# Attention's second stage: shares one step sooner, residual loads spread, last transposes and values one step sooner

## Chip, cores and metric

The kernel runs on one core of one Trainium2 chip, as one launch. The metric is the device time of a whole execution in microseconds, the median of several runs. Before the change it was 2018.47 us (three runs, 2016.84 to 2018.92).

## What is computed

Two layers of a decoder trunk over 1024 tokens of 1024 channels, all in float32: a gated short convolution, then a dilated sliding-window attention with 16 heads of 64 channels and three dilation groups. The change touches the attention layer only. There every head has three groups of queries, keys and values; each group gives an output and the logarithm of its softmax denominator, and the three outputs are added with weights (the shares) made from these denominators:

```python
def dilated_attention_mixer(h, w_in, q_gain, k_gain, w_out, rel_bias):
    proj = h @ w_in
    ...
    for g, (window, dilation) in enumerate(DILATED_GROUPS):   # (128, 1), (512, 4), (2048, 16)
        ...
        o, l = dilated_group_attention(q, k, qkv[:, :, g, 2], bias_g, window, dilation)
        outs.append(o)
        lses.append(l)
    alpha = jax.nn.softmax(jnp.stack(lses, axis=0), axis=0)
    o = jnp.sum(alpha[..., None] * jnp.stack(outs, axis=0).astype(jnp.float32), axis=0)
    y = o.reshape(B, S, ATTN_WIDTH).astype(h.dtype) * jax.nn.silu(z)
    return y @ w_out                                          # and x + y @ w_out is the result
```

## The kernel before

The first 1640 us compute the convolution layer and attention's projections. They leave queries and keys (`qkd`), values (`vd`), the SiLU gate (`zd`), the residual stream (`x1d`) and the skewed position biases (`sk0` to `sk2`) in device memory. From about 1640 us on runs the second stage, which alone is changed.

It treats the 16 heads as 8 pairs (`hp` 0 to 7), each pair as three units (`g` 0 to 2), and each unit as steps: 4, 4 and 2. So a pair has 10 steps and the stage 80, numbered 0 to 79; the last steps of the pairs are 9, 19, ... 79. A step has three parts, made by `make`:

- A: scores. TensorE multiplies queries and keys (L888, tile `ps`), VectorE adds the bias and takes the maximum (L896, tiles `xs` and `nl`), ScalarE takes the exponential and its sum (L899).
- B: TensorE transposes the probabilities (L906, tile `pt`); ScalarE or VectorE copies them to SBUF (L846, L844, tile `pts`).
- C: TensorE multiplies them with the values (L925, L919 for `g` 2, tile `po`); after a unit's last step VectorE copies the output out (`finish`, L936).

Engines run their instructions in the order in which the program was written. That order is fixed by hand: a loop counts k from 0, and at each k it issues every piece whose step plus lag is k. A has lag 0, B has lag `LB` = 2, C lag `LC` = 4. Within one k the lags come in the order 0, 1, 4, 3, 5 to 14, 2. After these come `extra` (the output projection, below) and `begins` (loads). Before all of them `add_sums` adds finished projections to the residual.

After a pair's last step (`end`) hangs a chain that joins its three groups; its pieces are functions inside `attention`, and their lags are counted from that last step:

- `store` (L942, L944, L947): `nl` of groups 0 and 1 goes to `nld` in device memory, in another order; at group 2 all of it is loaded back as `ml`. The DMAs are issued by GpSimd.
- `weights` (L956 to L960): maxima and exponentials on VectorE and ScalarE. `shares` (L969 to L974): the quotients, tile `fo`.
- `store_shares` (L977) sends them to `fd`, and `spread(w)` (L982, two DMAs) loads them back, repeated over 64 partitions, as `fb`. There are two `fb` buffers, so `spread(0)` waits for `scale(2)`.
- `scale(w)` (L985, VectorE, 1024 columns), `add(w)` (L988, GpSimd), `gate` (L991), `high` and `low` (L995, L998).

Before the change the lags of a pair that isn't the last are: `store` 1, `weights` 3, `shares`, `store_shares`, `spread(2)`, `spread(1)` 4, `scale(2)` and `spread(0)` 8, `scale(1)` and `add(2)` 9, `scale(0)` and `add(0)` 11, `gate` 12, `high` 13, `low` 14. GpSimd's queue holds these DMAs and the adds in that order, and an instruction that waits there holds up all behind it. So do the other engines' queues.

The last pair goes without device memory: `wide` (L1007, L1009) widens the shares on chip, `spread_last` (L1017) transposes them with TensorE into `ps` banks, and `last` multiplies, adds and gates half a row at a time.

The output projection lies between the steps: `some` multiplies two pairs' outputs with the output weights for one tile of 128 channels by 512 tokens, six matmuls (L1066 to L1068), in a PSUM bank (`pd`, of which there is one; `ps` has three, `pt` two, `po` two). There are three rounds of 16 such tiles: at k 34 to 49, at 54 to 69, and from 74 on, where six tiles are done by 79 and the rest at the stage's end, two to a k. `add_sums` (L1102) adds each to `acc`, which was loaded with the residual by `residual` (L1083, SyncE's queue) at k 4 to 19. `fetch`, `split` and `split_low` (L1077, L1080) prepare output weights. After the loop five tiles get pair 6's and 7's part in two goes (`first`), and eleven the whole.

The two lines that place the stores and the joining, and the one that places the loads:

```python
            end.setdefault(1, []).append(store)
...
                    todo = [(3, weights), (LC, shares), (LC, store_shares), (LC, lambda: spread(2)),
...
            when(4 + i, residual, dt, hf)
```

Of the kernel before, what the change touches and what calls it, by code (L numbers as in the profile page):

```python
# [35 lines left out]
def trunk(ctx: ExitStack, tc: tile.TileContext, a, out):  # L36
# [98 lines left out]
    with tc.tile_pool(name="wq", bufs=1) as wq, tc.tile_pool(name="sle", bufs=1) as sle, \  # L135
# [197 lines left out]
        with tc.tile_pool(name="rp", bufs=1, side="right") as rp, tc.tile_pool(name="cp", bufs=2, side="right") as cp, \  # L333
# [62 lines left out]
            with tc.manual_schedule(engines={mybir.EngineType.Activation}):  # L396
                ps, T = {}, {}
# [107 lines left out]
        with tc.tile_pool(name="ev", bufs=1, side="right", reuse_waits="tile") as ev, tc.tile_pool(name="xb", bufs=1, side="right", reuse_waits="tile") as xb, \  # L505
# [35 lines left out]
            WO, ps = {}, {}  # L541
# [268 lines left out]
    with tc.tile_pool(name="sp", bufs=3, space=PSUM) as sp, tc.tile_pool(name="ptp", bufs=2, space=PSUM) as ptp, \  # L810
# [37 lines left out]
        def attention(hp, g):  # L848
# [130 lines left out]
            def spread(w):  # L979
                fb = u["fb", w] = fbp.tile([P, S], F32, name="fb", tag="fb")  # L980
                for s, hs in enumerate((lo, up)):
                    nc.gpsimd.dma_start(fb[hs], fd[hp, w, s][None, :].to_broadcast([64, S]))  # L982

            def scale(w):
                nc.vector.tensor_tensor(O[hp, w], O[hp, w], u["fb", w], op=OP.mult)  # L985
# [25 lines left out]
            def spread_last(hf):  # L1011

                hs = slice(64 * hf, 64 * hf + 64)
                for w in (2, 1, 0):
                    fb = u["fb", w] = sp.tile([P, 4, P], F32, name="ps", tag="ps").rearrange("p a b -> p (a b)")
                    for r in range(8):
                        nc.tensor.transpose(fb.rearrange("p (i r) -> p r i", r=8)[:, r],  # L1017
                                            u["wide", w][hs, r * P:r * P + P], ident[hs, hs])

            def last(hf, i):  # L1020
                h, z = half(hf), SZ[hp][:, half(hf)]
                if i == 0:
                    for w in (2, 1, 0):
                        nc.vector.tensor_tensor(O[hp, w][:, h], O[hp, w][:, h], u["fb", w], op=OP.mult)
                elif i == 1:
                    for w in (2, 0):
                        nc.vector.tensor_tensor(O[hp, 1][:, h], O[hp, 1][:, h], O[hp, w][:, h], op=OP.add)
                    nc.vector.tensor_tensor(z, O[hp, 1][:, h], z, op=OP.mult)
                    if hf == 0:
                        y2[hp] = [ap.tile([P, S], F32R, name="qk", tag="qk", bufs=6) for _ in range(2)]  # L1030
                    nc.scalar.activation(y2[hp][0][:, h], z, AF.Copy)
                else:
                    nc.vector.tensor_tensor(y2[hp][1][:, h], z, y2[hp][0][:, h].bitcast(F32), op=OP.subtract)

            steps = []
# [3 lines left out]
                    st = make(js, not steps)  # L1039
                    steps.append({lag: [f] for lag, f in zip((0, LB, LC), st)})  # L1040
            end = steps[-1]
            end.setdefault(1, []).append(store)
            if g == 2:
                if hp == HP - 1:
                    todo = [(LB, weights), (3, shares), (3, wide), (LC, lambda: spread_last(0)),
                            (LC, lambda: last(0, 0)), (LC, lambda: last(0, 1))]
                    ending.update(spread=spread_last, last=last)
                else:
                    todo = [(3, weights), (LC, shares), (LC, store_shares), (LC, lambda: spread(2)),
                            (LC, lambda: spread(1)), (8, lambda: scale(2)), (8, lambda: spread(0)),  # L1050
                            (9, lambda: scale(1)), (9, lambda: add(2)), (11, lambda: scale(0)),
                            (11, lambda: add(0)), (12, gate), (13, high), (14, low)]
                for lag, f in todo:
                    end.setdefault(lag, []).append(f)
# [59 lines left out]
        def when(k, f, *x):  # L1114
            begins.setdefault(k, []).append(lambda: f(*x))
# [1 line left out]
        for un, (k, prefetch) in at.items():  # L1117
            when(max(0, k - 2), load_v, *un)
        for i, (dt, hf) in enumerate(tiles):
            when(4 + i, residual, dt, hf)  # L1120
        for r in range(3):
            k0 = at[2 * r + 2, 0][0] + LD
            k = k0
            for i, (dt, hf) in enumerate(tiles):
                late = k >= len(steps)
                name = "pd" if not late else ("pd", ("ps", "ps", "pt", "pt")[min(k - len(steps), 3)])[i % 2]
                extra.setdefault(k, []).append(lambda r=r, dt=dt, hf=hf, name=name:
                                               some((2 * r, 2 * r + 1), dt, hf, name))
                k += i % 2 if late else 1
        for kt in range(KT):  # L1130
            k = at[kt // 2 * 2 + 2, 0][0] + LD - 4 + kt % 2 if kt < 6 else len(steps) - 5 + kt % 2
            when(k - 4 - kt % 2, fetch, kt)
            when(k, split, kt)
            when(k + 1, split_low, kt)
        for f in begins.pop(-1):
            f()
        k = 0
        while k < len(steps) + LC or any(x >= k for x in extra):
            add_sums()
            for lag in (0, 1, LC, 3, *range(LC + 1, 15), LB):  # L1140
                for f in steps[k - lag].get(lag, ()) if 0 <= k - lag < len(steps) else ():
                    f()
            for f in extra.get(k, ()):
                f()
            for f in begins.get(k, ()):
                f()
            k += 1
# [94 lines left out]
```

## Time and profile before

| | us |
|---|---|
| median of three runs | 2018.47 |
| lowest, highest | 2016.84, 2018.92 |
| the profiled execution | 2009.19 |
| its span, first to last instruction | 2007.3 |
| TensorE busy in the span | 1948.4 (97%) |
| VectorE, ScalarE, GpSimd busy | 1482.8, 903.7, 881.5 |

The profile is one execution, about 9 us shorter than the median; differences are worked out on it and laid on the median. TensorE is busy 97% of the span; the rest are idle stretches, and within the busy time some stretches run at a lower granted clock. In the page's strip of 40 slices, TensorE shows 9 (90% or more) nearly everywhere; 8 stands in slices 35 to 38 and in the last one, that is in the stage that is changed and at the very end. A timeline row ends in square brackets when its engine sat idle before it: for how long, and which instruction ended the wait.

### The profile page before, as it was taken

What the parts mean: (1) busy time and instruction counts of PE and PEld (TensorE: products, weight loads), DVE (VectorE), ACT (ScalarE), POOL (GpSimd) and SP (SyncE); (2) the same over time, 40 slices, a digit from 0 to 9 for tenths busy, and PEclk for the clock granted to TensorE, in tenths of its full rate; (3) what the DMA queues carried; (4) which work ended last, traced back from release to release, by engine and by line L of the source; (5) the groups of instructions that cost most, each with busy time, mean ns of one, the idle gap of its engine ahead of it and who ended that gap; (6) DMA issues with size and microseconds to landing.
All of it is one profiled execution on the core that took longest, in us unless ns stands there. A gap on an engine that the chain in (4) does not pass through costs nothing.

```text
span 2007.3 us, 29480 instructions
## 1 busy us (share of the span) xinstructions
PE 1948.4 (97%) x10302; PEld 1583.3 (79%) x10302; DVE 1482.8 (74%) x2751; ACT 903.7 (45%) x2042; POOL 881.5 (44%) x800
## 2 busy tenths in 40 slices
PE   8999999999999999999999999999999998899998
PEld 6888778888888888788888888888888876677776
DVE  6866576566666655788889788968898856687886
ACT  5433233333334444444434443344333348777670
POOL 0356566666664211344445444544444441322230
PEclk9999999999999999999999999999999999999999
DMA  5326512122113564323333233323323368757752
GB/s 192 116 67 143 145 60 74 69 69 74 69 69 127 193 227 161 127 89 106 105 116 116 84 106 116 116 80 109 116 95 102 109 216 268 215 153 216 215 153 85
DMA packets 116805, 254.25 MB, mean 127 GB/s; under 512 B 15822, under 2 KB 22718, under 8 KB 116656
## 3 DMA queue, kind: packets, MB, share of 16 engines
q1 hardware_dynamic: 93024, 177.42, 26.9%
q0 software_dynamic: 23632, 74.95, 13.1%
q8 instruction: 81, 1.33, 0.3%
q14 instruction: 68, 0.56, 0.1%
HBM read 193.05 MB, written 67.64 MB: 130 GB/s over the span
## 4 chain that ended last, share of the span: by engine, by line
PE 66%; DVE 10%; issue 5%; DMA 2%; ACT 2%; POOL 1%; DVEq 0%; POOLq 0%; ACTq 0%; SPq 0%
PE pp L299 16%; PE pp L301 15%; PE pp L302 15%; PE pp L550 3%; PE pp L551 3%; PE pp L549 3%; PE ps L888 2%; DVE ws L165 2%; PE pt L906 2%; PE po L925 2%; DVE blkc L706 1%; DVE ri L67 1%; DMA nld<-nl 1%; ACT xs L899 1%; DVE st L670 1%
## 5 line engine op out<-in xcount | busy, mean ns | idle before, releaser
L165 DVE TENSOR_TENSOR ws<-wr,ws 128x512 fp32r<-128x512 f32 x284 | 268.4, 947 | 126.8 <-ACT ws L164 125.4
L164 ACT ACTIVATE ws<-wr 128x512 fp32r<-128x512 f32 x284 | 178.4, 630 | 389.5 <-PE pp L302 235.7
L164 ACT ACTIVATE ws<-sr 128x512 fp32r<-128x512 f32 x272 | 169.7, 629 | 293.8 <-PE pp L302 238.5
L274 POOL TENSOR_TENSOR sr<-wr 128x512 f32<-128x512 f32 x136 | 185.1, 1361 | 258.2 <-DVE rit L66 76.3
L165 DVE TENSOR_TENSOR ws<-sr,ws 128x512 fp32r<-128x512 f32 x272 | 235.7, 873 | 81.3 <-ACT ws L164 79.6
L311 DVE TENSOR_TENSOR f<-pp,f 128x512 f32<-128x512 f32 x204 | 139.5, 684 | 84.6 <-PE pp L302 80.0
L899 ACT ACTIVATE xs<-xs,nl 128x128 f32<-128x128 f32 (+1 forms) x384 | 167.9, 439 | 68.4 <-DVE nl L896 57.3
L307 ACT ACTIVATE f<-pp 128x512 f32<-128x512 f32 x228 | 132.5, 581 | 26.8 <-POOL blkc L678 12.9
L896 DVE CUSTOM_DVE_ANT_0 xs<-ps,bt 128x128 f32<-128x128 f32 (+1 forms) x384 | 110.8, 347 | 26.1 <-PE ps L888 16.4
L711 POOL DMA_DIRECT2D qkd<-blkc x96 | 68.1, 716 | 134.1 <-DVE blkc L706 126.7
L274 POOL TENSOR_TENSOR sr<-wr,sr 128x512 f32<-128x512 f32 x68 | 89.1, 1310 | 81.4 <-issue 57.7
L669 ACT ACTIVATE f<-f 128x512 f32<-128x512 f32 x96 | 60.7, 633 | 139.0 <-DVE f L311 101.8
L299 PE MATMUL pp<-blke,ws 128*128 128x512 f32 x272 | 108.2, 398 | 6.8 <-ACT f L307 6.8
L299 PE MATMUL pp<-blkg,ws 128*128 128x512 f32 x272 | 107.6, 396 | 4.6 <-ACT f L307 3.7
L301 PE MATMUL pp<-blkg,ws 128*128 128x512 f32 x272 | 106.8, 393 | 3.3 <-DVE blkg L519 3.3
L299 PE MATMUL pp<-blkf,ws 128*128 128x512 f32 x272 | 108.6, 399 | 0.7 <-ACT f L307 0.7
L299 PE MATMUL pp<-blka,ws 128*128 128x512 f32 x272 | 107.2, 394 | 0.7 <-ACT f L307 0.7
L299 PE MATMUL pp<-blkb,ws 128*128 128x512 f32 x272 | 107.5, 395 | 0.0
L301 PE MATMUL pp<-blke,ws 128*128 128x512 f32 x272 | 107.4, 395 | 0.0
L302 PE MATMUL pp<-blke,ws 128*128 128x512 f32 x272 | 107.1, 394 | 0.0
L299 PE MATMUL pp<-blkd,ws 128*128 128x512 f32 x272 | 107.0, 394 | 0.0
L302 PE MATMUL pp<-blkg,ws 128*128 128x512 f32 x272 | 106.5, 391 | 0.0
(329 smaller groups left out, 5387.6 us busy)
## 6 DMA issues: line engine op xcount, KB each, us to landing
wr<-in_conv_w_in SPq DMA_DIRECT2D x128, 256.0 KB, 2.8
wr<-in_wqk SPq DMA_DIRECT2D x96, 256.0 KB, 3.0
qkd<-blkc POOLq DMA_DIRECT2D x96, 256.0 KB, 3.1
qk<-qkd SPq DMA_DIRECT2D x48, 512.0 KB, 8.5
wr<-in_conv_w_out SPq DMA_DIRECT2D x64, 256.0 KB, 3.1
f<-in_x SPq DMA_DIRECT2D x48, 256.0 KB, 4.6
wr<-in_wv SPq DMA_DIRECT2D x48, 256.0 KB, 2.9
vd<-f POOLq DMA_DIRECT2D x48, 256.0 KB, 2.5
```

The costliest lines, as they stand in the source:

```text
L164: nc.scalar.activation(t[:, 0], src, AF.Copy)
L165: nc.vector.tensor_tensor(t[:, 1], src, t[:, 0].bitcast(F32), op=OP.subtract)
L274: nc.gpsimd.tensor_tensor(t, x, y, op=op)
L299: nc.tensor.matmul(ps, w[:, 0, ws], b[:, k, 0], start=new and k == 0, stop=False, skip_group_check=not new)
L301: nc.tensor.matmul(ps, w[:, 0, ws], b[:, k, 1], start=False, stop=False, skip_group_check=not new)
L302: nc.tensor.matmul(ps, w[:, 1, ws], b[:, k, 0], start=False, stop=end and k == 3, skip_group_check=not new)
L307: nc.scalar.activation(t, ps, AF.Copy)
L311: nc.vector.tensor_tensor(m, ps, m, op=OP.add)
L669: nc.scalar.activation(sq, t, AF.Square)
L711: nc.gpsimd.dma_start(qkd[hp, g, which].rearrange("p (c s) -> p c s", c=c) [:, :, hf * m:(hf + 1) * m], o.rearrange("p (c s) -> p c s", c=c))
L896: nc.vector.tensor_tensor_reduce(out=x, in0=ps[s][:, x0:x0 + nk].rearrange("p a b -> p (a b)"), in1=u["bt"][s][:, bs], op0=OP.add, op1=OP. ...
L899: nc.scalar.activation(x, x, AF.Exp, bias=nm, scale=-1.0, accum_out=L)
```

## The change

It moves pieces to other places and renames banks; it adds and removes no arithmetic.

- `store` of group 2 (the load of `ml`) from lag 1 to 0.
- For pairs 0 to 6: `weights` from lag 3 to 2 (at the end of that k, after B), `shares`, `store_shares`, `spread(2)` and `spread(1)` from 4 to 3.
- For pair 7: B of step 79 and `weights` go to the end of k = 80 (by `begins`), C of steps 78 and 79 from lag 4 to 3, `shares` and `wide` from 3 to 2, `spread_last(0)` and the first two parts of `last` from 4 to 3. The loop ends one k sooner.
- `residual` at k 6, 8, ... 36 in place of 4 to 19.
- In every round the tiles 14 and 15 use a `po` bank in place of `pd`; in the third round the last four tiles stand together at k = 83, with the banks in another order.

```diff
-            end.setdefault(1, []).append(store)
+            end.setdefault(0 if g == 2 else 1, []).append(store)
             if g == 2:
                 if hp == HP - 1:
-                    todo = [(LB, weights), (3, shares), (3, wide), (LC, lambda: spread_last(0)),
-                            (LC, lambda: last(0, 0)), (LC, lambda: last(0, 1))]
-                    ending.update(spread=spread_last, last=last)
+                    steps[-2][3] = steps[-2].pop(LC)
+                    end[3] = end.pop(LC)
+                    todo = [(2, shares), (2, wide), (3, lambda: spread_last(0)), (3, lambda: last(0, 0)),
+                            (3, lambda: last(0, 1))]
+                    ending.update(turn=end.pop(LB)[0], weights=weights, spread=spread_last, last=last)
                 else:
-                    todo = [(3, weights), (LC, shares), (LC, store_shares), (LC, lambda: spread(2)),
-                            (LC, lambda: spread(1)), (8, lambda: scale(2)), (8, lambda: spread(0)),
+                    todo = [(LB, weights), (3, shares), (3, store_shares), (3, lambda: spread(2)),
+                            (3, lambda: spread(1)), (8, lambda: scale(2)), (8, lambda: spread(0)),
...
-            when(4 + i, residual, dt, hf)
+            when(6 + 2 * i, residual, dt, hf)
...
-                name = "pd" if not late else ("pd", ("ps", "ps", "pt", "pt")[min(k - len(steps), 3)])[i % 2]
+                name = "pd" if not late else (("pd", "ps"), ("pd", "ps"), ("pd", "pt"), ("pt", "pd"))[
+                    min(k - len(steps), 3)][i % 2]
+                if i >= 14:
+                    name = "po"
...
-                k += i % 2 if late else 1
+                k += (i % 2 if i < 13 else 0) if late else 1
...
+        when(len(steps), ending["turn"])
+        when(len(steps), ending["weights"])
...
-        while k < len(steps) + LC or any(x >= k for x in extra):
+        while k < len(steps) + LC - 1 or any(x >= k for x in extra):
```

VectorE's queue at pair 2, from the gate of pair 1 (k = 31) to the scores of step 32. (`sz` is the gate's tile, `wraw` a raw output weight whose low part L1080 makes.) Before:

```order
L936 COPY o<-po 128x512
L991 TENSOR_TENSOR sz<-o,sz 128x1024
L1080 TENSOR_TENSOR y_14810<-wraw,y_14810 128x1024
L896 ISA xs,nl<-ps,bt 128x256
L896 ISA nl 128x1
```

The same place after the change:

```order
L991 TENSOR_TENSOR sz<-o,sz 128x1024
L956 TENSOR_TENSOR mx<-ml 128x16
L957 TENSOR_TENSOR mx<-mx,nl 128x16
L958 TENSOR_TENSOR f<-mx,ml 128x8x4
L959 TENSOR_TENSOR f<-mx,nl 128x8x2
L1082 TENSOR_TENSOR y_14807<-wraw,y_14807 128x1024
L896 ISA xs,nl<-ps,bt 128x256
L896 ISA nl 128x1
```

The four instructions of `weights`, the first of which needs `ml`, now stand ahead of the scores of step 32.

The same queue behind the scores of step 32. Before, the copies out of `po` at k = 33 (two L936) come next but four scores, and `shares` only behind them:

```order
L956 TENSOR_TENSOR mx<-ml 128x16
L957 TENSOR_TENSOR mx<-mx,nl 128x16
L958 TENSOR_TENSOR f<-mx,ml 128x8x4
L959 TENSOR_TENSOR f<-mx,nl 128x8x2
L844 COPY pts<-pt 128x384
L1080 TENSOR_TENSOR y_14853<-wraw,y_14853 128x1024
L896 ISA xs,nl<-ps,bt 128x256
```

After the change, VectorE behind the scores of step 32:

```order
L969 TENSOR_TENSOR den<-f,ml 128x8x4
L970 TENSOR_TENSOR den<-f,nl 128x8x2
L971 TENSOR_TENSOR den<-den 128x8x2
L972 TENSOR_TENSOR mx<-den 128x16
L973 RECIPROCAL mx<-mx 128x16
L974 TENSOR_TENSOR fo<-f,mx 128x8x6
L844 COPY pts<-pt 128x384
L1082 TENSOR_TENSOR y_14857<-wraw,y_14857 128x1024
L896 ISA xs,nl<-ps,bt 128x256
```

`shares` has moved from behind the scores and copies of k = 33 to ahead of the copy L844 of k = 32.

TensorE's queue at the end of k = 80 and the start of k = 81 (the first row is the end of a projection tile). Before:

```order
L1068 MATMUL ps<-y_17144,y_17097 128x512
L925 MATMUL po<-pts,V 64x128 x8
L906 MATMUL pt<-ident,xs 128x128 x8
L1066 MATMUL pd<-y_16575,y_17054 128x512
L1067 MATMUL pd<-y_16575,y_17054 128x512
```

After the change, TensorE from the end of the same projection tile on:

```order
L1070 MATMUL ps<-y_17159,y_17104 128x512
L906 MATMUL pt<-ident,xs 128x128 x8
L925 MATMUL po<-pts,V 64x128 x8
L919 MATMUL po<-pts,V 64x64 x16
L1068 MATMUL pd<-y_16590,y_17054 128x512
```

B of step 79 has moved ahead of C of step 77, and C of step 78 (L919) stands right behind that, with no projection between them. GpSimd's queue holds the same instructions in the same order before and after; only the loop's k differ.

## Rows read from the trace of the kernel before

**Rows 1.** Stretches: us, busy us (and instructions) of each engine, clock, DMA share, GB/s.

```profile
1685.00:1765.00 80.00, 67.14 (x702) 52.11 (x699) 57.15 (x253) 61.34 (x232) 23.51 (x26) 0.89 0.74 209
1765.00:1830.00 65.00, 65.00 (x599) 50.03 (x597) 52.23 (x211) 45.82 (x185) 20.56 (x24) 1.00 0.78 222
...
1950.00:1978.00 28.00, 24.86 (x201) 19.66 (x200) 20.13 (x40) 7.62 (x21) 2.77 (x2) 0.94 0.01 3
```

**Rows 2.** Timeline of TensorE: start, us, operation, [idle before, what ended it].

```profile
1702.59 2.07 PE L888 MATMUL ps<-qk 64*128 64x128 f32 x14 [4.21 <-DVE nl L896]
...
1740.11 2.07 PE L888 MATMUL ps<-qk 64*128 64x128 f32 x14 [3.88 <-DVE nl L896]
...
1758.22 1.61 PE L888 MATMUL ps<-qk 64*128 64x256 f32 x6 [2.99 <-DVE nl L896]
...
1845.50 0.88 PE L925 MATMUL po<-pts,V 128*64 128x128 f32 x12 [0.30 <-DVE o L936]
...
1952.62 1.14 PE L906 MATMUL pt<-ident,xs 128*128 128x128 f32 x8 [0.80 <-ACT pts L846]
...
1973.46 0.56 PE L1066 MATMUL pd<-y,y 128*128 128x512 f32 x1 [2.34 <-DVE acc L1102]
1973.82 0.63 PE L1067 MATMUL pd<-y,y 128*128 128x512 f32 x1
```

**Rows 3.** Timeline of VectorE, k = 12 to 23.

```profile
1681.12 0.17 DVE L956 TENSOR_TENSOR mx<-ml 128x16 f32<-128x16 f32 x1
...
1685.32 0.18 DVE L969 TENSOR_TENSOR den<-f,ml 128x32 f32<-128x32 f32 x1
...
1700.47 1.23 DVE L985 TENSOR_TENSOR o<-o,fb 128x1024 f32<-128x1024 f32 x1 [4.60 <-DMA fb<-fd]
...
1717.22 0.42 DVE L896 CUSTOM_DVE_ANT_0 xs<-ps,bt 128x256 f32<-128x256 f32 x1
...
1722.25 0.18 DVE L969 TENSOR_TENSOR den<-f,ml 128x32 f32<-128x32 f32 x1
```

**Rows 4.** Timeline of VectorE, k = 27 to 33.

```profile
1737.98 1.23 DVE L985 TENSOR_TENSOR o<-o,fb 128x1024 f32<-128x1024 f32 x1 [4.29 <-DMA fb<-fd]
...
1755.12 1.22 DVE L991 TENSOR_TENSOR sz<-o,sz 128x1024 f32<-128x1024 f32 x1 [2.59 <-POOL o L988]
...
1757.39 0.42 DVE L896 CUSTOM_DVE_ANT_0 xs<-ps,bt 128x256 f32<-128x256 f32 x1
...
1762.36 1.28 DVE L936 COPY o<-po 128x512 f32<-128x512 f32 x2
```

**Rows 5.** Timeline of GpSimd: issues of `nld` and `ml` for pairs 0, 2 and 4.

```profile
1674.37 0.56 POOL L942 DMA_DIRECT2D ml<-nld  x1 [6.86 <-issue]
...
1740.55 1.55 POOL L947 DMA_DIRECT2D nld<-nl  x2
...
1752.13 0.57 POOL L942 DMA_DIRECT2D ml<-nld  x1 [6.89 <-DVE nl L896]
...
1834.54 0.57 POOL L942 DMA_DIRECT2D ml<-nld  x1 [6.77 <-DVE o L985]
```

**Rows 6.** Tile `ml`, all pairs: its load, from issue to landing.

```profile
DMA to landing us min/median/max: 1.9/4.1/6.1
```

**Rows 7.** Tile `ml`, 1751 to 1753 us (pair 2).

```profile
DMA to landing us min/median/max: 5.4/5.4/5.4
```

**Rows 8.** Tile `fo`, all pairs: the store of the shares to `fd`.

```profile
DMA to landing us min/median/max: 2.5/3.5/6.7
```

**Rows 9.** Timeline of VectorE, k = 51 to 53.

```profile
1837.52 1.23 DVE L991 TENSOR_TENSOR sz<-o,sz 128x1024 f32<-128x1024 f32 x1 [0.59 <-POOL o L988]
...
1845.96 0.18 DVE L969 TENSOR_TENSOR den<-f,ml 128x32 f32<-128x32 f32 x1
...
1847.01 1.22 DVE L998 TENSOR_TENSOR y<-sz,y 128x1024 fp32r<-128x1024 f32 x1
```

**Rows 10.** Tile `ml`, 1833 to 1836 us (pair 4).

```profile
DMA to landing us min/median/max: 4.7/4.7/4.7
```

## The prediction

> **What bounds the kernel now.** I read the stretches of the stage first, then TensorE's timeline for its idle time, then the queue behind each wait. From 1765 to 1830 us TensorE is busy 65.00 of 65 us [rows 1]: where the projection lies between the steps it is the bound, and what is moved there costs nothing as long as it stays ahead. From 1685 to 1765 (k = 15 to 34, no projection yet) it is busy 67.14 of 80 us at a mean clock of 0.89, and from 1950 to 1978 24.86 of 28 us at 0.94 [rows 1]. All that can be won is there. In the first stretch the reader is to see three stops of 4.21, 3.88 and 2.99 us, each ended by VectorE's scores, with slow matmuls behind them [rows 2].
>
> VectorE does not lack time there. At 1700.47 and 1737.98 it had stood 4.60 and 4.29 us in front of `scale(2)` for the load of `fb` [rows 3, 4]. At 1755.12 it had stood 2.59 us at the gate for GpSimd's add [rows 4], and that add stood behind the load of `ml`, issued at 1752.13 after 6.89 us of waiting [rows 5]. The profile names VectorE for that last wait, but the instruction needs `nld`, stored at 1740.55 [rows 5], so I take it for that store's landing. So two loops of memory latency set this stretch: shares to `fd` to `fb` to `scale(2)`, and from `scale(2)` over the buffer of `spread(0)`, the `nld` store and `ml` to gate and `weights`, which starts the next one.
>
> **The change part by part. First loop, pair 0.** `shares` takes 1845.96 to 1847.01, 1.05 us [rows 9]. It began at 1685.32, so `fo` was there at 1686.4 and `scale(2)` could start at 1700.47 [rows 3], 14.1 us later. Now `shares` stands behind the scores of k = 12, which ended at 1681.12, where `weights` began [rows 3]; `fo` is there at 1682.2, `fb` at 1696.3, and VectorE comes there at 1700.47 - 4.60 = 1695.9. So the 4.60 us wait falls to 0.4, unless `weights` waits: it now stands ahead of those scores, from about 1681.1 - 1.4 (four scores) - 0.6 (four instructions of 0.17 us with their gaps) = 1679.1, and `ml` lands at 1674.37 + 6.1 = 1680.5 at the latest [rows 5, 6]. That costs 0 to 1.4 us; I take half. `scale(2)` at 1697.0, 3.5 us sooner.
>
> **Then pair 1.** From `scale(2)` to the scores of k = 22 there were 1717.22 - 1700.47 = 16.75 us [rows 3], set by the second loop, and I keep them; `weights` now stands in between, 0.6 more. These scores start at 1714.35, 2.9 sooner. `fo` came at 1722.25 + 1.05 = 1723.3, 6.1 us after their start [rows 3]; now 1.4 + 1.05 = 2.45 after it: 1716.8, 6.5 sooner. From `fo` to `scale(2)` were 14.7 us [rows 4], so 1731.5. VectorE comes there about 3.5 us sooner than at 1733.7 (2.9, and `weights` done already), and waits 1.3 where it waited 4.29.
>
> **Then pair 2.** The gate follows 6.5 us sooner, at 1748.6, and ends at 1749.8. `ml` was issued at 1752.13 and took 5.4 [rows 5, 7]; 6.5 sooner it lands at 1751.0. `weights` now waits 1.2 us for it, in front of the scores, and these wait with it, ScalarE's exponentials and TensorE's next scores too. Scores of k = 32: 1751.0 + 0.6 + 1.1 (the split L1080) = 1752.7, where they were at 1757.39 [rows 4]. The copies out of `po`, which TensorE's values of k = 34 need, came 4.97 us behind them, at 1762.36 [rows 4]. Now 1.4 + 1.05 + 0.5 + 1.1 + 1.4 = 5.45 behind (scores, shares, copy, split, scores): 1758.2. **From here TensorE is 4.2 us ahead**, of the 6.5 to 8.9 that the two `fb` waits seemed to promise: what is late next is `nld`, `ml` and the add behind them. From both sides: 0, if `nld` and `fb` land later by as much as the moved residual loads add; 10, if the landings shrink with the earlier issue.
>
> **Residual loads.** 16 loads of 256 KB; pair 0's steps lose about five, those of k = 20 to 36 gain nine. No queue but SyncE's is touched and each load has 13 steps or more before its use. Their price is in the landings: `fd` took 2.5 to 6.7 us [rows 8], and `ml` 1.9 to 6.1 [rows 6]. Lighter traffic in pair 0 (up to 1.4 us, above) stands against heavier in pairs 1 and 2; I let them cancel, plus or minus 2. The Trainium skill ("DMA: Bandwidth & Descriptors", section "Queues, rings and completion order") says that each DMA engine goes round robin between queue rows. By it GpSimd's small transfers share with SyncE's row however many loads lie in that row, so thinning a full row gains nothing in pair 0, while loads put where the row was empty cost; the sum would be some 1 us worse. No row here tells the two apart.
>
> **Pairs 3 to 6.** In pairs 3 and 5 projections run, and the same shift stays behind TensorE's work: nothing. Pairs 4 and 6 end between two rounds (k = 50 to 53), where VectorE runs without a gap from the gate on, and TensorE waited 0.30 us for the copy out of `po` (and the same at pair 6) [rows 2]. There `shares`, 1.05 us, moves ahead of that copy: 1.05 us lost in each pair. At pair 4 `ml` lands at 1834.54 + 4.7 = 1839.2 [rows 5, 10], and the gate ends at 1837.52 + 1.23 = 1838.75 [rows 9]: 0.5 us more. Loss 2.6 us; between 0 (if VectorE's later queue takes it up) and 4. The tiles 14 and 15 in `po`: tile 15 must now wait for the copy at k = 49 and 69, about 1 us, and TensorE waits anyway for the chain at k = 51 and after: nothing.
>
> **The end.** TensorE stood 0.80 us at 1952.62 for ScalarE's copy, which stays. It stood 2.34 us at 1973.46 for the single `pd` bank, whose add was queued behind `last` on VectorE, and its next nine matmuls came every 0.43 us in place of 0.23 (one of them was 0.63 long), since the clock fell [rows 2]: 1.7 us. With shares and `last` one k earlier and the last four tiles in three kinds of bank that goes: 4.0 us. New: C of step 78 stands right behind C of step 77 and needs its `po` copy, 0.64 us (half of the pair L936) [rows 4] and what VectorE has in hand: 0.9 us; and about 0.3 at k = 83 for `pd`. **Gain 2.8 us**, between 1 and 4.
>
> **The sum.** 4.2 + 2.8 - 2.6 = 4.4 us. The profiled execution took 2009.19 us (span 2007.3 and 1.9 around it) and would take 2004.8; on the median, 2018.5 - 4.4 = 2014.1.
>
> **The rivals.** (a) *The second loop swallows the first stretch's gain.* The scores of k = 32 hang on `ml` now, and pair 2's landings grow with the loads put there. Then the first term is 0 to 2, and with the end and pairs 4 and 6 it comes to 2017 to 2018.5. For: VectorE's 2.59 us at the gate are this loop already. Against: its start, `scale(2)`, does come sooner. (b) *The `fb` waits were all.* Landings shrink as issues leave the bursts. Then the first term is near 10 and the time 2008 to 2010. For: `ml` landed in 1.9 us at best. Against: the DMA engines are busy 0.74 of that stretch [rows 1], and must move the same bytes in less time. (c) *Slower: VectorE waits for `ml` in front of the scores.* `weights` lost one step of slack in seven pairs. In pairs 1, 2, 4 and 6 nothing covers that wait. If `ml` lands 2.2 us later there than reckoned (by its end of range against its median [rows 6] about this much), four times 2.2 = 8.8 us go against 4.4 of gain: 2022.9. It decides from 1.1 us on, where the gain is gone. (d) *The change does not do what it says*: GpSimd's queue keeps its order, and the moved `ml` load waits for `nld` as before, so that piece alone is worth nothing; the shares do move, and I count this under (a).
>
> **How the numbers follow.** Forecast, 2011 to 2016: 0.45. (a): 0.25. (b): 0.18. (c): 0.12. A measurement of this kernel can tell 0.2%, about 4 us, from no change: faster means below 2014.4. The forecast lies on that edge, a little over half of it below; with (b) and some of its own lower side I give faster 0.47, same 0.43, slower 0.10. The range must leave out no more than 0.2: it takes in (a) and the near part of (b) and leaves out the far end of (b) and (c): 2008.5 to 2020.
>
> **What would show it.** Right: no wait above 2 us for `fb` at `scale(2)` of pairs 0 and 1; a wait for `ml` (VectorE at L956, named so or as idle time there) ahead of the scores of k = 32; TensorE's values at k = 34 some 4 us sooner; an idle gap below 1 us at C of step 78 and none of 2 us in k = 84's place; 0.5 to 2 us more idle time at k = 52 to 54 and 72 to 74. Wrong: gate and scores of k = 22 and 32 not sooner though `scale(2)` is (a), or both sooner by more than 6 us (b), or L956 waiting 2 us or more in pairs 4 and 6 (c).

## The result, and the profile after

The changed kernel took 2008.71 us (median of six, 2004.63 to 2012.25) where the kernel before, beside it, took 2018.36 (2016.11 to 2022.30): ratio 0.995, interval 0.9933 to 0.9967, which is 6.7 to 13.5 us. The forecast was 4.4 us (2014.1) and the range, 2008.5 to 2020, just reaches the result: right sign, less than half the size. One execution of the kernel before, at 2412.4 us and a granted clock of 0.752, is left out of every number below. The changed kernel's profiled execution took 2010.56 us (span 2008.8), which is *longer* than that of before (2009.19). So the two traces must be laid on each other where the stage begins. TensorE's timeline of the changed kernel has the first scores here (start, us, operation):

```profile
1646.44 1.35 PE L888 MATMUL ps<-qk 64*128 64x128 f32 x10
```

In before they stand at 1642.39: the unchanged part ahead ran 4.05 us longer by chance. Below, "moved back" means that 4.05 is taken off a time of after.

On the page of before, TensorE is under 90% busy in the slices 1, 34, 35 and 40, not in 35 to 38: 34 and 35 are 1656 to 1756 us, so the stage's lost time lies mostly at its start. TensorE's idle time after the change, the rows that answer to [rows 2]:

```profile
1720.36 1.13 PE L888 MATMUL ps<-qk 64*128 64x256 f32 x6 [2.11 <-DVE nl L896]
...
1758.73 1.30 PE L888 MATMUL ps<-qk 64*128 64x256 f32 x6 [3.44 <-DVE nl L896]
...
1842.65 2.07 PE L888 MATMUL ps<-qk 64*128 64x256 f32 x6 [2.91 <-DVE nl L896]
...
1930.73 0.88 PE L925 MATMUL po<-pts,V 128*64 128x128 f32 x12 [0.58 <-DVE o L936]
...
1956.50 1.14 PE L906 MATMUL pt<-ident,xs 128*128 128x128 f32 x8 [0.80 <-ACT pts L846]
1963.08 1.15 PE L919 MATMUL po<-pts,V 128*64 128x64 f32 x30 [0.69 <-DVE o L936]
```

At pair 4 the kernel before has this:

```profile
1840.62 1.13 PE L888 MATMUL ps<-qk 64*128 64x256 f32 x6 [0.90 <-DVE nl L896]
```

The stops of 4.21 and 3.88 us are gone, with a smaller one in between (2.11, at k = 22); that at k = 32 is still there (3.44), the stop at pair 4 has grown from 0.90 to 2.91, and at the end the 2.34 us in front of `pd` is gone and 0.69 stands at the values of step 78. VectorE, the rows that answer to [rows 3, 4]:

```profile
1683.61 0.17 DVE L956 TENSOR_TENSOR mx<-ml 128x16 f32<-128x16 f32 x1 [0.89 <-DMA ml<-nld]
...
1699.96 1.22 DVE L985 TENSOR_TENSOR o<-o,fb 128x1024 f32<-128x1024 f32 x1
...
1711.64 1.23 DVE L985 TENSOR_TENSOR o<-o,fb 128x1024 f32<-128x1024 f32 x1 [3.10 <-DMA fb<-fd]
...
1736.21 1.21 DVE L985 TENSOR_TENSOR o<-o,fb 128x1024 f32<-128x1024 f32 x1
...
1748.49 1.23 DVE L985 TENSOR_TENSOR o<-o,fb 128x1024 f32<-128x1024 f32 x1 [4.25 <-DMA fb<-fd]
1753.20 1.22 DVE L991 TENSOR_TENSOR sz<-o,sz 128x1024 f32<-128x1024 f32 x1 [0.91 <-POOL o L988]
1756.16 0.17 DVE L956 TENSOR_TENSOR mx<-ml 128x16 f32<-128x16 f32 x1 [1.73 <-DMA ml<-nld]
...
1757.90 0.41 DVE L896 CUSTOM_DVE_ANT_0 xs<-ps,bt 128x256 f32<-128x256 f32 x1
...
1763.31 1.28 DVE L936 COPY o<-po 128x512 f32<-128x512 f32 x2
```

The reader is to see where the waits went. At `scale(2)` (1699.96, 1736.21) nothing waits for `fb` any more; at `scale(0)` (1711.64, 1748.49) VectorE now waits 3.10 and 4.25 us for it, where it had waited 1.12 and 1.40 (below); and `weights` waits 1.73 us for `ml` ahead of the scores of k = 32. `scale(0)` of the same pairs before the change:

```profile
1710.91 1.22 DVE L985 TENSOR_TENSOR o<-o,fb 128x1024 f32<-128x1024 f32 x1 [1.12 <-DMA fb<-fd]
...
1748.72 1.23 DVE L985 TENSOR_TENSOR o<-o,fb 128x1024 f32<-128x1024 f32 x1 [1.40 <-DMA fb<-fd]
```

The loads of `fb` for `scale(0)` are issued when `scale(2)` has freed the buffer, as GpSimd's timeline shows:

```profile
1701.47 1.04 POOL L982 DMA_DIRECT2D fb<-fd  x2 [8.36 <-DVE nl L896]
...
1737.74 1.04 POOL L982 DMA_DIRECT2D fb<-fd  x2 [8.43 <-DVE nl L896]
...
1750.21 0.57 POOL L942 DMA_DIRECT2D ml<-nld  x1 [7.50 <-DVE o L985]
```

From issue to use pass 10.2 and 10.8 us. This is the second loop of the prediction, and it is what is late next. Two stretches after the change, columns as in [rows 1]. The first is the end, 4 us longer than in [rows 1]; the second is the early 80 us, moved by 4:

```profile
1950.00:1982.00 32.00, 30.52 (x255) 24.69 (x254) 25.51 (x58) 11.06 (x37) 5.29 (x3) 1.00 0.02 5
1689.00:1769.00 80.00, 67.21 (x734) 52.00 (x732) 60.30 (x265) 64.53 (x245) 26.54 (x31) 0.96 0.83 233
```

TensorE is as long busy in the early 80 us as before (67.21 after, 67.14 before) but does 734 instructions where it did 702, at a mean clock of 0.96 in place of 0.89. At the end the clock is 1.00 where it was 0.94.

### The profile page after: what moved, and what is told of

Same layout as the page of the kernel before. It is cut to its first block, busy times and chain, and to the rows that moved or that the text cites. A ratio compares the mean times of both kernels' runs of the same rounds, so it can differ in the third digit from the quotient of the medians.

```text
span 2008.8 us, 29492 instructions
## 1 busy us (share of the span) xinstructions
PE 1948.2 (97%) x10302; PEld 1583.2 (79%) x10302; DVE 1473.5 (73%) x2751; ACT 904.3 (45%) x2042; POOL 882.2 (44%) x800
## 4 chain that ended last, share of the span: by engine, by line
PE 66%; DVE 10%; issue 4%; DMA 3%; ACT 2%; POOL 1%; SPq 0%; DVEq 0%; POOLq 0%; ACTq 0%
PE pp L299 16%; PE pp L302 15%; PE pp L301 15%; PE pp L550 3%; PE pp L551 3%; PE pp L549 3%; DVE ws L165 2%; PE pt L906 2%; PE ps L888 2%; PE po L925 1%; DVE blkc L706 1%; ACT xs L899 1%; DVE st L670 1%; DVE ri L67 1%; DMA nld<-nl 1%
## 5 line engine op out<-in xcount | busy, mean ns | idle before, releaser
L165 DVE TENSOR_TENSOR ws<-wr,ws 128x512 fp32r<-128x512 f32 x284 | 260.2, 918 | 134.4 <-ACT ws L164 132.9
L165 DVE TENSOR_TENSOR ws<-sr,ws 128x512 fp32r<-128x512 f32 x272 | 231.0, 856 | 88.6 <-ACT ws L164 87.0
L896 DVE CUSTOM_DVE_ANT_0 xs<-ps,bt 128x128 f32<-128x128 f32 (+1 forms) x384 | 110.8, 347 | 25.0 <-PE ps L888 17.6
```

Of the source, the lines that this page charges most:

```text
L165: nc.vector.tensor_tensor(t[:, 1], src, t[:, 0].bitcast(F32), op=OP.subtract)
L896: nc.vector.tensor_tensor_reduce(out=x, in0=ps[s][:, x0:x0 + nk].rearrange("p a b -> p (a b)"), in1=u["bt"][s][:, bs], op0=OP.add, op1=OP. ...
```

## The experiments

Single executions of one kernel spread by 2 to 3.4 us (standard deviation), so the runs were pooled. Over four sets, each on another chip, the kernel before had 144 executions, mean 2015.1 us; the sets' own means are 2014.7 to 2016.2. Each difference below is a kernel's mean less the 2015.1, with twice its standard error behind it; the number ahead of it is the kernel's own median. Taken against the same set's executions of before alone, no difference changes by more than 0.5 us, but for the two filled kernels (below). A second reading comes from TensorE's timeline of each trace and does without the part ahead of the stage: from the first scores to the first projection matmul (k = 34), from the last matmul of a round of the projection to the first of the next (pair 4: k = 50 to 53, pair 6: k = 70 to 73; these two are called gaps), and from the last scores to the end of the span. All are in us.

| kernel (traces) | to k = 34 | pair 4 | pair 6 | end |
|---|---|---|---|---|
| before (4) | 122.8, 121.7, 121.7, 125.4 | 18.4, 19.3, 19.0, 20.8 | 17.6, 17.5, 17.9, 17.8 | 59.5, 59.8, 59.5, 58.0 |
| after (4) | 119.5, 120.3, 116.9, 120.8 | 21.0, 20.4, 19.5, 21.0 | 18.2, 17.5, 17.4, 17.4 | 57.1, 55.7, 57.2, 57.3 |
| difference of means | -3.5 | +1.1 | -0.1 | -2.4 |
| forecast | -4.2 | +1.6 | +1.0 | -2.8 |
| joining alone | 120.6 | 20.2 | 17.4 | 60.8 |
| joining, pairs 0 to 3 | 121.5 | 18.8 | 18.9 | 59.5 |
| end alone (2) | 123.4, 125.2 | 18.8, 20.7 | 17.7, 17.8 | 56.0, 57.2 |
| residual alone | 124.4 | 19.4 | 17.9 | 58.3 |
| after, pairs 4 and 6 late (2) | 116.4, 117.2 | 16.6, 17.9 | 16.4, 16.8 | 56.1, 56.0 |
| the same without the spread | 117.8 | 17.4 | 16.9 | 57.3 |
| before, filled | 122.6 | 20.5 | 17.7 | 60.8 |
| after, filled | 117.6 | 20.2 | 17.4 | 55.6 |

**The kernel before, again** (no edit), three times.

> The kernel before, unchanged, for a second trace of it and the spread between executions. The profiled execution of before took 2009.2 us, 9 us under its median; against it the changed kernel's stage is 2.5 us shorter, while the medians differ by 9.7. Theory 1 (the stage): the usual execution of before loses some 5 to 7 us more in the stage than the profiled one did, by more or longer stretches at the low clock behind the three stops at 1700, 1738 and 1755 us; then this trace, if it is of a usual length (2014 to 2020), shows the stage start at 1640 to 1645 us and the stage 5 us or more longer than the 365 us of before. Theory 2 (elsewhere): the extra time lies ahead of 1640 us, where nothing was changed; then the stage starts 4 to 9 us later and is as long as before. Ratio 1.000.

> The kernel before, unchanged, for a third trace. From the first scores to the end, its two traces so far took 364.9 and 364.8 us, the changed kernel's two 362.4 and 360.5, 3.4 us less; the medians of the times differ by 7.5 to 9.7. Both traces of before come from executions below their median (by 9.3 and 1.9 us). Theory 1 (the stage of before is usually longer than those two traces): this trace has a stage of 366 to 370 us, with one or two slow stretches more. Theory 2 (the start of the stage, 1642.4 and 1644.5 us in those two traces, is what made them short, and it differs by chance alone): stage 365 again, and the start anywhere from 1642 to 1650 us.

> The kernel before, unchanged, in the changed kernel's place. Theory (a bias of the place): 0.9988 again, 2 us under the shared runs of before, stage 364.5 to 365 us. Rival (chance): 1.000 within 0.0005.

Medians 2013.1, 2013.9 and 2014.7; ratios to the other executions of before 0.9988, 0.9988 and 0.9997. The bias of the place that I suspected after two of them is not there. From the first scores to the end they took 364.8, 364.6 and 368.6 us (364.9 in the trace of before), the first scores stood at 1644.5, 1647.8 and 1644.8: a good part of the spread between executions lies ahead of the stage, in code that no kernel here changes.

**The changed kernel, again** (no edit), three times.

> The changed kernel, unchanged, beside the kernel before on one chip, in twice as many executions, for the size of the gain and a second trace. So far: 9.7 us at the median of six; the three parts alone gave 4.3, 1.9 and 1.0 at the median of 12. Theory 1 (clock): of what the change gains, 5 us is TensorE's lost time at the low clock (share of clock lost times the time: 24.7 us in before, 19.4 in the six executions of after), and the rest is 2 to 4 us of waits; then before minus after is 7 to 9 us here, the mean granted clock 0.990 against 0.988. Theory 2 (my prediction's terms, the large number was chance): 4.4 us, ratio 0.998, and no more than 2 us of it in the clock.

> The changed kernel, unchanged, for a third trace and more times. Theory 1: stage 358 to 361 us, and before minus after 8 to 9 us over all executions. Theory 2: stage 361 to 362 us; over all executions 5 to 7 us.

> The changed kernel, unchanged. Theory (the forecast's 4.4 us is the size, the rest was place and chance): 4 to 6 us under e13, stage 359 to 362 us. Rival (the recorded 9.7 is the size): 8 us or more under e13, stage under 357 us.

Medians 2008.5, 2009.1 and 2008.0, ratios 0.9959, 0.997 and 0.9962. Thirty executions against 144: **-6.8 +- 1.2 us**, between the two expectations of the last run (4 to 6, or 8 and more). About 3 us of the recorded 9.65 do not come back: the six executions of before had a median of 2018.36, the 144 have 2014.8, while after stays at 2008.7. The forecast's 4.4 is 2.4 us short of that. The traces' pieces add up to -4.9, with 2 us or more of spread in them.

**One part at a time.** The joining of pairs 0 to 6 alone:

```diff
-            end.setdefault(1, []).append(store)
+            end.setdefault(0 if g == 2 and hp < HP - 1 else 1, []).append(store)
...
-                    todo = [(3, weights), (LC, shares), (LC, store_shares), (LC, lambda: spread(2)),
-                            (LC, lambda: spread(1)), (8, lambda: scale(2)), (8, lambda: spread(0)),
+                    todo = [(LB, weights), (3, shares), (3, store_shares), (3, lambda: spread(2)),
+                            (3, lambda: spread(1)), (8, lambda: scale(2)), (8, lambda: spread(0)),
```

> Before with only the joining of pairs 0 to 6 moved (the load of ml one k sooner, weights at lag 2, shares, their store and the loads of fb at lag 3). The prediction's terms: 4.2 us gained up to k = 34, 2.6 lost in pairs 4 and 6, so 2016.8 of 2018.4 (ratio 0.999). Rival b (the fb waits were all): 8 to 10 gained up to k = 34, 2010 to 2013 (ratio 0.996). Rival a (ml and nld swallow it): 2018 to 2021 (1.000 to 1.001).

Median 2011.0, -4.4 +- 2.0, where the prediction's terms gave 1.6 (4.2 less 2.6) and rival (b) 8 to 10. Then the same in pairs 0 to 3 alone (`t` is 1 for pairs 4, 5 and 6; their `ml` is still loaded one k sooner):

```diff
+                    t = 1 if hp in (4, 5, 6) else 0
+                    todo = [(LB + t, weights), (3 + t, shares), (3 + t, store_shares), (3 + t, lambda: spread(2)),
+                            (3 + t, lambda: spread(1)), (8, lambda: scale(2)), (8, lambda: spread(0)),
```

> Before with the joining moved in pairs 0 to 3 alone (and ml loaded one k sooner everywhere); residual's loads, pairs 4 to 6 and the end as before. The prediction's first term alone: 4.2 us gained, all of it ahead of k = 34 (2011.5 where before has 2015.7). Rival: 7 us (2008.5), since the moved joining of all pairs gave 4.8 and the late pairs 4 and 6 took another 2.3 off the changed kernel, and part of it is then clock, not chain.

Median 2009.9, -4.5 +- 1.3: the size of the first term, 4.2 (pair 3's gain, below, is in it too), and the 7 us of the rival are not there. The two kernels are equal (0.1 +- 2.3), where 2.6 us of loss was reckoned for moving pairs 4 to 6 as well. But not because nothing is lost there. The gap at pair 6 in the kernel with pairs 0 to 3 alone, TensorE's last matmul of the round first, then VectorE:

```profile
1916.37 0.40 PE L1069 MATMUL pd<-y,y 128*128 128x512 f32 x1
1919.96 1.23 DVE L985 TENSOR_TENSOR o<-o,fb 128x1024 f32<-128x1024 f32 x1 [1.01 <-DMA fb<-fd]
...
1925.18 1.23 DVE L991 TENSOR_TENSOR sz<-o,sz 128x1024 f32<-128x1024 f32 x1 [1.42 <-POOL o L988]
...
1932.42 1.28 DVE L936 COPY o<-po 128x512 f32<-128x512 f32 x2
```

And with the joining of all pairs 0 to 6 moved:

```profile
1915.43 0.40 PE L1068 MATMUL pd<-y,y 128*128 128x512 f32 x1
1917.92 1.22 DVE L985 TENSOR_TENSOR o<-o,fb 128x1024 f32<-128x1024 f32 x1
...
1921.92 1.22 DVE L991 TENSOR_TENSOR sz<-o,sz 128x1024 f32<-128x1024 f32 x1
...
1930.20 1.28 DVE L936 COPY o<-po 128x512 f32<-128x512 f32 x2
```

The gate in this gap (L991) is that of the pair before, pair 5. With pair 5's joining moved, `scale(0)` no longer waits for `fb` nor the gate for GpSimd's add, and the gate starts 6.49 us behind the round in place of 8.81. From the gate to the copies out of `po` pass 8.28 us in place of 7.24, since the shares of pair 6 now stand ahead of them. One pair gains what the next one loses. All 18 traces, filled ones too, divide the same way, with an overlap of 0.05 us in one place, the first two columns at pair 4 (mean, lowest to highest, us; in the first two columns it counts whether the joining of the pair before, 3 or 5, was moved, in the last two whether the gap's own pair's was):

| gap at | round's end to gate: moved | not moved | gate to copies: moved | not moved |
|---|---|---|---|---|
| pair 4 | 7.8 (6.7 to 8.6) | 9.0 (8.5 to 9.3) | 9.5 (8.7 to 10.1) | 7.24 (7.23 to 7.24) |
| pair 6 | 6.7 (6.5 to 7.2) | 8.0 (7.7 to 8.8) | 8.3 (8.28 to 8.30) | 7.24 (7.23 to 7.24) |

The end alone (pair 7's lines, the banks and the loop's bound, as in the diff of the change), twice:

> Before with only the last pair's change and the banks of the projection tiles (transposes and weights of step 79 at the end of k = 80, values of steps 78 and 79 and the last shares one k sooner, tiles 14 and 15 in po, the last four tiles at k = 83). The prediction's term: 2.8 us gained (1 to 4), 2015.6 of 2018.4 (ratio 0.9986), all of it behind 1950 us. Rival: the end holds more of the gain than that, 5 to 7 us (ratio 0.997), because the usual execution loses the clock at 1970 us for longer than the profiled one did.

> Before with only the end changed, as before under another label. Theory (the end's term is real, 2.8 to 3.3 us): 2.5 to 3.5 us under e13, the end from the last scores 56 to 57 us against 59.5. Rival (the end gains in the trace what is lost ahead of it): less than 1 us under e13.

Medians 2013.4 and 2011.2, together -2.1 +- 1.3. In all ten traces that have its change the end is 1.9 to 3.5 us shorter than the mean of before, 59.2. The residual's loads alone (`when(6 + 2 * i, ...)`):

> Before with only the residual's loads spread over k = 6 to 36. The prediction: 0 plus or minus 2 us (ratio 0.999 to 1.001). Rival (the moved loads are the gain that was missed): the landings of ml and of the shares in pairs 0 and 1 come back to 2 to 3 us, the stops at 1702 and 1740 us shrink by 3 us each and the time falls by 4 to 6 us (ratio 0.997 to 0.998). Rival (round robin between queue rows, loads put where the row was empty): 1 us slower (1.0005).

Median 2014.2, -0.4 +- 1.4: nothing. The parts (the joining of all pairs, the end, the loads) add up to 4.4 + 2.1 + 0.4 = 6.9 us, the whole gave 6.8.

**Work put into the stops.** Is it the stop that costs, or the slow matmuls behind it? Both kernels were filled so that TensorE stands less:

```diff
             add_sums()
+            if k in FILL:
+                pd = bank("pd")
+                for i in range(FILL[k]):
+                    nc.tensor.transpose(pd[:, i % 4 * P:i % 4 * P + P], ident, ident)
```

> The kernel before with work added that no result needs: TensorE transposes the identity into the idle bank pd, 16 times ahead of the scores of k = 19, 16 ahead of those of k = 29 and 12 ahead of those of k = 32 (about 2.3, 2.3 and 1.7 us), which lies inside the three stops of 4.2, 3.9 and 3.0 us. No wait is removed. Theory (the clock behind the stops is a large part of what the change gains): the three slow stretches go or shrink, the mean clock rises by 0.001 to 0.002 and the time falls by 2 to 4 us. Rival (only the waits count, slow matmuls behind a stop are hidden since VectorE bounds that stretch): time within 1 us of before, whatever the clock does; and if the stops are shorter in other executions, up to 2 us slower.

> The changed kernel with the same filling in its three longest stops: 12 transposes of the identity ahead of the scores of k = 22, 16 ahead of those of k = 32 and 16 ahead of those of k = 52 (stops of 2.11, 3.44 and 2.91 us in its trace). Theory: the slow stretches at 1720, 1760 and 1840 us go, mean clock 0.991 to 0.992, 2 to 3 us under the changed kernel. Rival: within 1 us of it.

Before, filled: median 2014.0, -0.8 +- 1.5. At the first stop TensorE's timeline shows the added transposes (L1144), half the stop left, and slow transposes behind it all the same (granted clock 0.61 from 1702 to 1708 us):

```profile
1697.20 1.91 PE L1144 MATMUL pd<-ident 128*128 128x128 f32 x16
1699.04 0.48 PE L888 MATMUL ps<-qk 64*128 64x128 f32 x2
1701.54 1.16 PE L888 MATMUL ps<-qk 64*128 64x128 f32 x14 [2.01 <-DVE nl L896]
...
1704.76 1.97 PE L906 MATMUL pt<-ident,xs 128*128 128x128 f32 x8 [1.48 <-DVE pts L844]
```

After, filled: median 2006.4, 1.3 +- 2.1 under the changed kernel. The mean granted clock rose from 0.9881 to 0.9900 and from 0.9904 to 0.9922, which is 3.9 and 3.6 us less lost to the low clock (the share lost times each execution's time). The times fell by 0.8 and 1.3 us, neither clear of its uncertainty; against their own set alone by 1.9 +- 2.1 and 0.3 +- 2.6, so that the 2 us of the expectation are not ruled out. At the third stop of before the filling left 1.03 us of idle time and the clock stayed at 1.00 (1755 to 1765 us), yet k = 34 starts at 122.6, no sooner than in before. So the early stops seem to cost as waits, and the slow matmuls behind them to be mostly hidden behind the engine that is waited for; that they cost nothing is not shown. The lost share counts idle time too: in before, TensorE does nothing from 1698.4 to 1702.5 us, at a granted clock of 0.78.

**Pairs 4 and 6 at the old lags**, the rest as changed (`t` as above, for pairs 4 and 6), twice, and once more with the residual's loads back at k = 4 to 19:

> The changed kernel with the old lags for weights and shares (3 and 4) in pairs 4 and 6 alone. The trace of after shows TensorE stopping 2.91 us at k = 52 where before it stopped 0.90, with slow matmuls behind it, and 3 us of its lead lost between k = 32 and k = 72. Theory: the lead of 3.5 us is kept through pairs 4 and 6 and the time falls 2 to 4 us under the changed kernel (ratio to before 0.993 to 0.995). Rival: the lead is given back elsewhere (TensorE waits for the same fb and ml later), then it is within 1 us of the changed kernel.

> The changed kernel with the old lags for weights and shares in pairs 4 and 6, as before. Theory (shares ahead of the copies cost TensorE 2 to 3 us there): 2.5 to 3 us under e14, the gaps between the projection's rounds 16.5 to 17.5 us against 20 and 17.6. Rival (its first trace was a lucky one): within 1 us of e14.

> The changed kernel with the residual's loads back at k = 4 to 19 and the old lags for weights and shares in pairs 4 and 6. In the trace of the changed kernel on this second occasion TensorE stopped 4.87 us at 1747.39 for the load of queries and keys, in that with late pairs 4 and 6 2.52 us at 1741.76: a wait that no trace without the spread loads shows. Theory (the spread costs what its loads push back, since they stand in the same queue as the queries and keys): that wait is gone, the start of k = 34 comes 1 to 3 us sooner than in the changed kernel (119 to 120 us behind the first scores), and the time is 2003 to 2005 where the changed kernel has 2008. Rival (the spread pays in pairs 0 and 1 what it costs in pair 2): within 1 us of the kernel that has late pairs 4 and 6 and the spread, 2005 to 2006.

The load of `ml` stays one k sooner in all three. Medians 2005.8, 2005.3 and 2006.5; ratios to before 0.9954 (0.9938 to 0.9969), 0.995 (0.9932 to 0.9968) and 0.9954 (0.9936 to 0.9972). The first two together are 3.3 +- 2.0 us under the changed kernel: **this version beats both**, and by -10.1 +- 1.7 us the kernel before. VectorE at pair 4 in the changed kernel, from the gate on:

```profile
1837.38 1.23 DVE L991 TENSOR_TENSOR sz<-o,sz 128x1024 f32<-128x1024 f32 x1 [0.78 <-POOL o L988]
1840.08 0.18 DVE L956 TENSOR_TENSOR mx<-ml 128x16 f32<-128x16 f32 x1 [1.47 <-DMA ml<-nld]
...
1841.83 0.41 DVE L896 CUSTOM_DVE_ANT_0 xs<-ps,bt 128x256 f32<-128x256 f32 x1
...
1843.20 0.18 DVE L969 TENSOR_TENSOR den<-f,ml 128x32 f32<-128x32 f32 x1
...
1847.23 1.28 DVE L936 COPY o<-po 128x512 f32<-128x512 f32 x2
```

And in the second run of the version with pairs 4 and 6 late:

```profile
1834.05 1.22 DVE L991 TENSOR_TENSOR sz<-o,sz 128x1024 f32<-128x1024 f32 x1 [1.42 <-POOL o L988]
...
1836.32 0.42 DVE L896 CUSTOM_DVE_ANT_0 xs<-ps,bt 128x256 f32<-128x256 f32 x1
...
1837.70 0.17 DVE L956 TENSOR_TENSOR mx<-ml 128x16 f32<-128x16 f32 x1
...
1841.28 1.28 DVE L936 COPY o<-po 128x512 f32<-128x512 f32 x2
...
1842.48 0.18 DVE L969 TENSOR_TENSOR den<-f,ml 128x32 f32<-128x32 f32 x1
```

From the gate to the scores pass 4.45 us in the one and 2.27 in the other, from the gate to the copies out of `po` 9.85 and 7.23. The difference of 2.6 us is the 1.47 of waiting for `ml` and the 1.05 of `shares` ahead of the copies. The wait is the mechanism of rival (c), at one pair and at 1.5 us. The gaps of the three traces are 17.3 and 16.7 us in the mean, against 20.5 and 17.6 in the changed kernel and 19.4 and 17.7 in before: this version keeps the sooner gates of pairs 3 and 5 and does not pay for those of 4 and 6. It is not the banks of the tiles 14 and 15, which the end alone has too, with gaps as in before. That its first two traces reach k = 34 some 2.6 us sooner than the changed kernel's is chance, since up to there the two programs are the same; both come from the fastest execution that the kernel had in its set. Taking the spread back as well changed nothing that can be told (+1.2 +- 2.2), so the expected 1 to 3 us of the spread's price are not seen.

That expectation came from a wait for queries and keys. TensorE in the trace of the changed kernel's second repeat has it too:

```profile
1747.49 1.65 PE L888 MATMUL ps<-qk 64*128 64x128 f32 x8 [4.18 <-DMA qk<-qkd]
...
1757.84 1.03 PE L906 MATMUL pt<-ident,xs 128*128 128x128 f32 x6 [0.16 <-ACT pts L846]
```

It stands at the scores of pair 3, for loads that there took 12.3 and 15.1 us to land. It appeared in four of the seven traces that have the spread and the moved joining together (0.56 to 4.87 us), and in none of the eleven that lack one of them (over 0.4 us). But where it is longer than 2 us the stop at k = 32 is gone, as the second row shows (the next idle time, 0.16 us), and k = 34 starts no later (116.9 us in this trace, 119.5 in the one with the stop): one wait takes the place of another.

## Why the prediction was right or wrong

**First loop: right, and a little better than forecast.** `weights` waited 0.89 for `ml` (0 to 1.4 was given), `scale(2)` of pair 0 came at 1699.96, 1695.9 moved back, where I had 1697.0 and 0.4 of waiting. What I had not seen: the store of the shares lands faster for being issued one step sooner. Tile `fo`, all pairs, after the change [rows 8]:

```profile
DMA to landing us min/median/max: 2.4/2.4/2.9
```

At pair 0 it took 6.4 to 7.9 us in the eight traces with the old place, the residual-alone kernel among them (6.7), and 2.4 or 2.5 in the ten with the new one, spread or not. What it avoids are other transfers. The 2.5 us behind its issue, before the change and after it (columns as in [rows 1]):

```profile
1686.80:1689.30 2.50, 2.50 (x32) 2.04 (x31) 2.40 (x16) 2.46 (x12) 0.82 (x1) 1.00 0.93 338
```

```profile
1687.06:1689.56 2.50, 2.50 (x43) 2.14 (x41) 2.50 (x11) 2.00 (x9) 0.84 (x1) 1.00 0.32 61
```

The DMA engines are 0.92 to 1.00 busy there in the eight traces, 0.32 to 0.36 in the ten. The first load of `fb` behind the store now meets that traffic instead: it landed after 3.6 to 5.4 us in the eight and takes 6.8 to 7.9 in the ten. So of the 4.5 us that the store gains in the mean, that load gives 3.0 back.

**Pairs 1 and 2: the chain held, within 1.2 us at each step.** I kept 16.75 us from `scale(2)` to the scores of k = 22; it became longer, because `scale(0)` now waits for its `fb`. The shares of pair 1 started at 1716.9 moved back (forecast 1715.75), `scale(2)` at 1732.2 (1731.5), the gate at 1749.2 (1748.6), `weights` at 1752.1 (1751.0, with 1.73 of waiting for 1.2), the scores of k = 32 at 1753.9 (1752.7), the copies that the values of k = 34 need at 1759.3 (1758.2): 3.1 us sooner than before for 4.2 forecast, 3.5 in four traces each, 4.5 by the times of the kernel with pairs 0 to 3 alone (whose one trace has only 1.4). Rival (a) did not come, and rival (b), which gave the measured time, did not come either as a mechanism: the `fb` wait moved from `scale(2)` to `scale(0)` and `ml` stayed late.

**Residual loads: right**, at nothing (-0.4 +- 1.4). The landings at pair 0 hardly came down (`ml` 4.8 to 5.6 us in eight traces with the spread, 5.2 to 6.4 in ten without). By the Trainium skill ("DMA: Bandwidth & Descriptors", section "Queues, rings and completion order") each DMA engine goes round robin between the queue rows that it has work for, so that a shorter row of SyncE's leaves GpSimd's turn as it is; these landings agree with it, and the 1 us of loss that I drew from it is not seen, though it lies at the edge of the uncertainty.

**Pairs 3 to 6: the step that failed.** The price of pairs 4 and 6, 2.6 us, was there and a little more: from the gate to the copies 1.05 us more at pair 6 (1.05 forecast) and 2.3 more at pair 4 (1.55 forecast, with 0.5 for `ml`; the wait for it was 0.3 to 1.7 in four traces). What failed is the term beside it: in pairs 3 and 5 the same shift "stays behind TensorE's work: nothing". The gates of pairs 3 and 5 lie at k = 51 and 71, in the very gaps where TensorE waits for VectorE, and they came 1.2 and 1.3 us sooner: 2.5 us of gain that the sum put at nothing. So pair 6's gap stayed as long as it was (-0.1), pair 4's grew by 1.1 and not by 1.55. With the 2.5 the prediction's sum is 6.9 us, with the measured price (3.35) as well it is 6.2; 6.8 +- 1.2 was measured. The kernel with pairs 4 and 6 late has the gain without the price, and was 3.3 +- 2.0 us faster than the changed one.

**The end: right.** 2.8 forecast, 2.4 by the traces, 2.1 by the times. The new wait at step 78 took 0.69 for 0.9, the `pd` stop and the slow matmuls behind it are gone.

**The last step**, from the sum to the median, held no term for the spread of the measurement itself: the median of six that the kernel before was given lay 3.5 us above that of 144. Of the 5.25 us between the forecast 4.4 and the recorded 9.65, 2.85 are this, which is chance, and 2.4 are left for the step above.

## What to carry to other kernels

When a chain of memory round trips is moved sooner, follow each buffer: the wait for `fb` went from the first user of the buffers to the one that reuses one. Follow each moved chain also to where its last piece lands: the gates of pairs 3 and 5, whose joining ran unseen behind the projection, stood in the next gap. A piece moved for a stretch that waits should be moved there alone; in the stretches that are bound by the moved piece's own engine, leaving it late was worth 3 us. And where single executions spread by 3 us, a change of 5 us is sized from pieces of several traces laid on a common point of the program and from some thirty times, not from one trace and six.

## What the runs showed of the hardware

The identical code ahead of the stage took from 1641.8 to 1651.4 us in 18 traces (to the first scores). A small store can land in a third of the time when it is issued 4 us sooner, ahead of other traffic: the store of pair 0's shares took 2.4 us with the DMA engines 0.32 busy and 6.7 with 0.93, and the loads behind it paid part of that. And a higher mean granted clock need not be as much time won: filling the stops of before gave 0.9900 for 0.9881, 3.9 us less lost to the low clock, and the time fell by 0.8 +- 1.5 us.
